# Splitting the transfers of a hybrid decoder block between SyncE's and ScalarE's DMA queues

## The chip, the cores and the metric

The kernel runs on one core of a Trainium2 chip, in one launch. The metric is the device time of the execution in microseconds (us). A core has five engines with programs of their own: TensorE (PE, with its weight loads PEld), VectorE (DVE), ScalarE (ACT), GpSimd (POOL) and SyncE (SP). Each works through its program in order. An engine's program can also hold instructions that start a DMA transfer; here they are said to stand in that engine's queue. The transfers themselves are carried out by 16 DMA engines. Engines and transfers wait for each other by semaphores.

## What is computed

The reference is one decoder block on 1024 tokens of width 1024 in float32. Two kinds of attention run on parallel head groups: A is grouped-query attention in a causal window of 128 with a sink in the softmax, 8 query heads on 2 key/value heads of 64; B mixes three dilated causal windows over 8 heads of 64. Cut to what matters:

```python
mod = cond @ w_ada + b_ada                         # cond = silu(c); six rows of 1024
sh_a, sc_a, gt_a, sh_m, sc_m, gt_m = split(mod, 6)
h = rms_norm(x, g_attn_pre) * (1 + sc_a) + sh_a
proj = h @ w_in                                    # 1024 x 2304: q, k, v of A, then of B
oa = banded_attention(rope(qa), rope(ka), va, 127, sink=sink_a)
ob = dilated_mixture_attention(rope(qb), rope(kb), vb)
y = concat(rms_norm(oa, g_mix_a), rms_norm(ob, g_mix_b)) @ w_out
x = x + gt_a * rms_norm(y, g_attn_post)
h = rms_norm(x, g_mlp_pre) * (1 + sc_m) + sh_m
y = square(relu(h @ w_up)) @ w_down                # 1024 -> 4096 -> 1024
x = x + gt_m * rms_norm(y, g_mlp_post)
```

## The kernel before

Matrices are multiplied in float32 precision out of two parts: a value is split into a high part, rounded to the type that TensorE takes, and the low part that is left, and each product is three matmuls (high by high, high by low, low by high). So each operand of TensorE is first cast by ScalarE (the high part) and subtracted by DVE or POOL (the low part).

The stages, as they start: load x and the first weights, norm and transposes; the input projection in six units (u = 0, 1 for A, 2 to 5 for B), each of which reads six blocks of w_in (128 x 512 values each); attention items, which run while later units are still projected (for A an item is one of 8 query blocks of one key/value head, in three parts: scores, exponentials and transposes, products with v); the output projection with post-norm and the input of the MLP, in eight blocks of 128 rows (the "output stage"); the MLP.

*The planner.* `Sched` fixes the order of each engine's program when the kernel is built. Each piece of work is an `op` with an engine, an estimated duration, the pieces it needs (`deps`), the buffers that it takes and gives back (`takes`, `gives`, counted by a `Res`), and a priority. The planner keeps a clock for each engine and gives out the piece that its estimates say is ready. `load` is the piece for a transfer: it stands on SyncE, its issue is priced at 0.62 us for each DMA instruction (`n`), and its end at the end of a running sum of transfer times, `self.dma`, plus 0.8. `e = op("ACT", ...)` and the like give the event that others name in their `deps`.

*The transfers.* All of the 533 DMA instructions stand in SyncE's queue. Those that matter here, by line:
- `load_w` (L530): a block of w_in, 256 KB, into the buffer `w_st`. `split_w` (L539 on ScalarE, L544 on DVE or POOL) makes `w_hl` of it, and the second of these gives `w_st` back. Unit 0's blocks are loaded in a hand-written order ahead of all (`prio is None`); the others are given a priority.
- `f_st` (L803): the rotated and split q and k of a unit go from the stage buffer `hl` to other partitions, into the tiles `qt` and `kt`. This is a transfer within the core's memory. For q of A, high and low parts are separate pieces (`s_` is 0 and 1), with one DMA instruction for each head and half in a piece. `hl` is written by L763 or L774 on ScalarE (high part) and L766 or L777 on POOL or DVE (low part). Scores (L1177 for A, L1122 for B) read `kt` and `qt`.
- `ada_piece` (L994): a piece of w_ada, 512 KB, into `wa_st`, for the modulation rows that are needed later; POOL multiplies and adds it up (L1005 to L1010). Its pieces with i below `NADA` (24) run beside the attention, the later ones in the MLP stage. L1034 and L1035 load rows of b_ada and of the post-norm's gain into `gate_st`.
- `open_attention` (L971): the masks, once.
- L1314 (A) and L1296 (B): an attention result from `ot` to `o_dram`, which the output stage reads back. `ot` (L1309, L1293 on DVE) is made out of `otmp` (L1304, L1289 on ScalarE), a copy of the products with v.
- L1343: w_out in eight pieces of 512 KB into `wo_st`. L1418 reads `o_dram` back; L1422 reads the rows of x for the residual, `x_sb2`, 512 KB.
- L1641: the raw blocks of w_up and w_down; the first four of these pairs are read in the output stage.

`wa_st`, `gate_st`, `wo_st`, `x_sb2` and `hl` are all tiles of one ring of stage buffers (`stage`, `r_stg`).

On ScalarE, in the attention stage, stand the casts of w (L539) and hl (L763, L774), copies of v (L825, `vt`; L839, `v_hl`), tables for the rotation (L721), exponentials (L1197 for A, L1148 for B), casts of transposed probabilities (`ph`, L1241) and the copies `otmp`. TensorE's projection writes `pj` (L861 to L864); it transposes v with L831 (`pv`) and the probabilities with L1227 to L1234 (`pt_ps`), and L1257 to L1269 are the products with v (`o_ps`).

## Time and profile before

| | us |
|---|---|
| median of 3 runs | 1166.8 |
| lowest and highest of them | 1165.25, 1167.23 |
| the profiled execution, whole | 1161.99 |
| its span, first to last instruction | 1160.2 |
| mean clock granted to TensorE in it | 0.986 of full speed |

| engine | work in the attention and output stages |
|---|---|
| TensorE | projections, scores, transposes, products |
| ScalarE | high parts, exponentials, copies out of the accumulators |
| DVE | rotation, low parts, maxima, sums |
| POOL | low parts, division of the probabilities, modulation rows |
| SyncE | all transfers |

The slices of the page, 29 us each, show the stages by the transfers: the line "GB/s" has 351 in the first slice, where x and the first weights come in, 102 to 182 while attention and projection run together, and then rises and falls with the blocks of the MLP.

How to read the rows that follow: times are in microseconds from the span's start, "x8" is a count, and an arrow "<-" gives what ended an idle time. SPq is SyncE's queue; a time beside it is the time that an instruction took to be issued there, its waits not counted unless they fell into it. In a chain, "DMA kt<-hl" is a transfer from its issue to its landing. PEclk is the clock granted to TensorE as a share of full speed.

### The profile page before, as it was taken

What the parts mean: (1) busy time and instruction counts of PE and PEld (TensorE: products, weight loads), DVE (VectorE), ACT (ScalarE), POOL (GpSimd) and SP (SyncE); (2) the same over time, 40 slices, a digit from 0 to 9 for tenths busy, and PEclk for the clock granted to TensorE, in tenths of its full rate; (3) what the DMA queues carried; (4) which work ended last, traced back from release to release, by engine and by line L of the source; (5) the groups of instructions that cost most, each with busy time, mean ns of one, the idle gap of its engine ahead of it and who ended that gap; (6) DMA issues with size and microseconds to landing.
All of it is one profiled execution on the core that took longest, in us unless ns stands there. A gap on an engine that the chain in (4) does not pass through costs nothing.

```text
span 1160.2 us, 15646 instructions
## 1 busy us (share of the span) xinstructions
PE 1117.1 (96%) x5416; PEld 926.6 (80%) x5416; DVE 815.4 (70%) x1380; ACT 639.2 (55%) x1105; POOL 261.1 (23%) x344
## 2 busy tenths in 40 slices
PE   8989989999999899998999999999999999999996
PEld 7768778788888787887788888888888888888885
DVE  7848576566666775658969665499653796547998
ACT  7949676455555774667676524563233732246542
POOL 2347667566663441112000000000000000000002
PEclk9989989999999989999999999999999999999998
DMA  9477857465545614554683057812369212585103
GB/s 351 161 174 168 168 120 182 111 153 122 134 102 130 156 48 139 193 181 182 257 314 118 19 207 274 315 50 89 120 220 326 106 55 73 184 306 181 37 19 146
DMA packets 90944, 185.31 MB, mean 160 GB/s; under 512 B 8432, under 2 KB 31088, under 8 KB 90864
## 3 DMA queue, kind: packets, MB, share of 16 engines
q1 hardware_dynamic: 90864, 184.30, 51.1%
q8 instruction: 43, 0.70, 0.3%
q14 instruction: 37, 0.30, 0.1%
HBM read 137.08 MB, written 28.31 MB: 143 GB/s over the span
## 4 chain that ended last, share of the span: by engine, by line
PE 70%; DVE 10%; DMA 7%; issue 4%; POOL 4%; ACT 3%; SPq 2%; DVEq 0%; POOLq 0%; ACTq 0%
PE mlp_ps L1898 16%; PE mlp_ps L1899 16%; PE mlp_ps L1897 16%; PE pj L861 3%; PE pj L864 3%; PE pj L862 3%; PE s_ps L1122 2%; PE o_ps L1257 1%; DMA wa<-in_w_ada 1%; SPq L803 1%; PE pt_ps L1227 1%; DMA wa_st<-in_w_ada 1%; DVE hw L1668 1%; PE pt_ps L1230 1%; PE s_ps L1177 1%
## 5 line engine op out<-in xcount | busy, mean ns | idle before, releaser
L1897 PE MATMUL mlp_ps<-hw 128*128 128x512 f32 x896 | 349.7, 390 | 1.2 <-ACT hw L1659 1.2
L1898 PE MATMUL mlp_ps<-hw 128*128 128x512 f32 x896 | 348.7, 389 | 1.1 <-DVE hw L1665 1.1
L1899 PE MATMUL mlp_ps<-hw 128*128 128x512 f32 x896 | 348.6, 389 | 0.0
L1897 PEld LDWEIGHTS mlp_ps<-hw 128*128 128x128 f32 x896 | 168.2, 188 | 36.8 <-ACT hw L1659 1.6
L1898 PEld LDWEIGHTS mlp_ps<-hw 128*128 128x128 f32 x896 | 168.2, 188 | 36.8 <-DVE hw L1665 1.4
L1899 PEld LDWEIGHTS mlp_ps<-hw 128*128 128x128 f32 x896 | 168.2, 188 | 34.9
L1668 DVE TENSOR_TENSOR hw<-w,hw 128x1024 fp32r<-128x1024 f32 x96 | 114.5, 1219 | 94.7 <-ACT hw L1661 94.4
L1661 ACT CAST hw<-w 128x1024 fp32r<-128x1024 f32 x96 | 97.5, 1047 | 129.8 <-PE mlp_ps L1899 97.5
L1997 POOL TENSOR_TENSOR st<-st,nhalf 128x1 f32<-128x1 f32 x8 | 7.8, 978 | 601.9 <-DVE st L1995 601.9
L861 PE MATMUL pj<-hw,w_hl 128*128 128x512 f32 x240 | 104.2, 434 | 0.0
L864 PE MATMUL pj<-hw,w_hl 128*128 128x512 f32 x240 | 95.5, 398 | 0.0
L862 PE MATMUL pj<-hw,w_hl 128*128 128x512 f32 x240 | 95.3, 397 | 0.0
L1245 DVE TENSOR_TENSOR ph<-pt_ps,ph 128x512 fp32r<-128x512 f32 (+1 forms) x110 | 69.7, 648 | 36.0 <-ACT ph L1241 35.7
L1661 ACT CAST hw<-u 128x1024 fp32r<-128x1024 f32 x48 | 48.7, 1052 | 64.6 <-PE mlp_ps L1899 64.6
L1241 ACT CAST ph<-pt_ps 128x512 fp32r<-128x512 f32 (+1 forms) x110 | 59.5, 555 | 32.1 <-PE pt_ps L1230 27.0
L1668 DVE TENSOR_TENSOR hw<-u,hw 128x1024 fp32r<-128x1024 f32 x48 | 57.0, 1218 | 18.2 <-ACT hw L1661 18.2
L1148 ACT ACTIVATE p_sb<-p_sb,mn 128x128 f32<-128x128 f32 (+3 forms) x64 | 49.7, 777 | 36.3 <-DVE mn L1141 34.9
L1955 DVE TENSOR_TENSOR yacc<-yacc,mlp_ps 128x512 f32<-128x512 f32 x96 | 62.1, 681 | 3.3 <-PE mlp_ps L1899 3.3
L1153 POOL TENSOR_SCALAR p_sb<-p_sb,den 128x128 f32<-128x128 f32 (+3 forms) x64 | 49.0, 775 | 47.8 <-DVE den L1151 44.6
L1010 POOL TENSOR_TENSOR ada_acc<-ada_acc,wa_st 128x512 f32<-128x512 f32 x42 | 55.5, 1320 | 3.5
L864 PEld LDWEIGHTS pj<-hw,w_hl 128*128 128x128 f32 x240 | 45.6, 190 | 10.7
L1473 PE MATMUL y_ps<-hw,oh 128*128 128x512 f32 x128 | 51.7, 404 | 0.0
(205 smaller groups left out, 2010.6 us busy)
## 6 DMA issues: line engine op xcount, KB each, us to landing
hw<-s_dram SPq DMA_DIRECT2D x84, 512.0 KB
wa_st<-in_w_ada SPq DMA_DIRECT2D x32, 512.0 KB
w<-in_w_up SPq DMA_DIRECT2D x32, 512.0 KB
w<-in_w_down SPq DMA_DIRECT2D x32, 512.0 KB
s_dram<-hw SPq DMA_DIRECT2D x28, 512.0 KB
w_st<-in_w_in SPq DMA_DIRECT2D x36, 256.0 KB
x_sb<-in_x SPq DMA_DIRECT2D x16, 512.0 KB
wa<-in_w_ada SPq DMA_DIRECT2D x32, 256.0 KB
```

What stands on the lines that cost most here:

```text
L861: T.matmul(ps, w[:, 0, n], h[0], start=(k == 0), stop=False)
L862: T.matmul(ps, w[:, 1, n], h[0], start=False, stop=False)
L864: T.matmul(ps, w[:, 0, n], h[1], start=False, stop=(k == KC - 1))
L1010: G.tensor_tensor(ada.acc[:, :512], ada.acc[:, :512], wa[:, j], ALU.add)
L1241: A.copy(b["ph"][:, 0, :w], b["pt"][:, :w])
L1245: V.tensor_tensor(b["ph"][:, 1, :w], b["pt"][:, :w], b["ph"][:, 0, :w].bitcast(F32), ALU.subtract)
L1661: A.copy(out[j][0], flat(src[j]))
L1668: V.tensor_tensor(out[j][1], flat(src[j]), out[j][0].bitcast(F32), ALU.subtract)
L1897: T.matmul(ps[m][:], sh, mh, start=starts and k == 0, stop=False, **kw)
L1898: T.matmul(ps[m][:], sh, ml_, start=False, stop=False, **kw)
L1899: T.matmul(ps[m][:], sl, mh, start=False, stop=k == 3, **kw)
L1955: e = op("DVE", t_dv(512), lambda: V.tensor_tensor(y(), y(), ps[m][:], ALU.add), [e, ml.e_y[tb, n]], gives=gives, prio=1)
```

## The change

103 of the DMA instructions go to ScalarE's queue (`nc.scalar.dma_start`), the others stay on SyncE's:
- `w_st` of units 1 to 5 (30);
- the high parts of A's q (20; the low parts and k stay);
- `wa_st` with i below 24 (24) and the four loads of `gate_st` among them;
- the masks (1), `wo_st` (8), `x_sb2` (8), and of the raw weights the halves with h = 0 (8).

The planner gets three kinds of transfer. "bulk" is what goes to ScalarE apart from q: it is ready `SLACK` (0.8 us) later than its needs are met, takes `ISSUE` (0.5 us) of ScalarE for each DMA instruction, and ends by the sum `self.dma`. "small" (q, k, `o_dram`, the reads of `o_dram`, the stores of x2) ends by a sum of its own, `self.few`, whichever queue it stands in. All others are priced as before. The different prices also move other pieces in the order of each engine's program a little, and which of DVE and POOL makes some of the low parts.

```diff
--- before.py
+++ after.py
@@ -149,6 +149,9 @@
 PW = 0.0
 
 
+SLACK, ISSUE = 0.8, 0.5
+
+
 class Ev:
 
     __slots__ = ("t", "eng")
@@ -181,7 +184,7 @@
         self.pe = {}
         self.launch = []
         self.seq = 0
-        self.dma = 0.0
+        self.dma = self.few = 0.0
         self.filler = None
 
     def step(self, dur, emit, deps=(), takes=(), gives=(), prio=5, after=None, kind="", n=1):
@@ -213,10 +216,11 @@
 
     def ready(self, o, e):
         t = 0.0
+        late = SLACK if e == "ACT" and o.kind == "bulk" else 0.0
         for d in o.deps:
             if d.t is None:
                 return None
-            x = d.t + lat(d.eng, e)
+            x = d.t + lat(d.eng, e) + late
             if x > t:
                 t = x
         for r, n in o.takes:
@@ -224,7 +228,7 @@
                 continue
             if len(r.free) < n:
                 return None
-            x = sorted(r.free)[n - 1]
+            x = sorted(r.free)[n - 1] + late
             if x > t:
                 t = x
         return t
@@ -236,10 +240,19 @@
             del r.free[:n]
         emit()
         end = start + dur
-        if e == "SP":
+        if e == "SP" and o.kind != "small":
             self.clk[e] = start + 0.62 * o.n
             self.dma = max(self.dma, start + 1.1) + max(dur, 0.62 * (o.n - 1))
             end = self.dma + 0.8
+        elif o.kind == "bulk":
+            self.clk[e] = start + ISSUE * o.n
+            self.dma = max(self.dma, start + 1.1) + dur
+            end = self.dma + 0.8
+        elif o.kind == "small":
+            each = 0.62 if e == "SP" else ISSUE
+            self.clk[e] = start + each * o.n
+            self.few = max(self.few, start + 1.1) + max(dur, each * (o.n - 1))
+            end = self.few + 0.8
         else:
             self.clk[e] = end
         o.ev.t = end
@@ -446,8 +459,9 @@
             return ring_r(name)
         return st.stgp.tile([P, 1024], F32, name=name, tag="stg")
 
-    def load(emit, nbytes, deps=(), takes=(), prio=5, gives=(), after=None, n=1):
-        return op("SP", nbytes / (345e3 if prio > -500 else 370e3), emit, deps, takes=takes, prio=prio, gives=gives, after=after, n=n)
+    def load(emit, nbytes, deps=(), takes=(), prio=5, gives=(), after=None, n=1, q="SP", kind=""):
+        return op(q, nbytes / (345e3 if prio > -500 else 370e3), emit, deps, takes=takes, prio=prio, gives=gives, after=after,
+                  n=n, kind=kind)
 
     def rsqrt_mean(dst, src, dep):
         box = []
@@ -527,11 +541,11 @@
     def load_w(u, i, prio=None, deps=()):
         def emit():
             t = w_raw[u, i] = prp.tile([P, 512], F32, name="w_st", tag="w_st", bufs=WS)
-            nc.sync.dma_start(t[:], w_in[6 * u + i])
+            (nc.sync if prio is None else nc.scalar).dma_start(t[:], w_in[6 * u + i])
         if prio is None:
             w_rawe[u, i] = in_turn(emit, 262144, r_wst)
         else:
-            w_rawe[u, i] = load(emit, 262144, deps, takes=[(r_wst, 1)], prio=prio)
+            w_rawe[u, i] = load(emit, 262144, deps, takes=[(r_wst, 1)], prio=prio, q="ACT", kind="bulk")
 
     def split_w(*a):
         def hi():
@@ -787,9 +801,10 @@
                 both = isb == (whose == "q")
                 nh = 2 if isb else 4 if whose == "q" else 1
                 for s_ in ((0, 1) if not both else (None,)):
+                    eng = nc.scalar if s_ == 0 and not isb else nc.sync
                     new = c == 0 and whose == "k" and s_ in (0, None)
 
-                    def f_st(s_=s_, new=new, mine=mine, whose=whose, nh=nh, both=both):
+                    def f_st(s_=s_, new=new, mine=mine, whose=whose, nh=nh, both=both, eng=eng):
                         if new:
                             if not x:
                                 ks[u] = kring.tile([P, 2, 1024], F32R, name="kt", tag="kt")
@@ -800,7 +815,7 @@
                             m_ = n_ // nh
                             for i in range(2) if both else (s_,):
                                 o = dst[64 * i + row:64 * i + row + m_].bitcast(F32)
-                                nc.sync.dma_start(o, src if both else src[:, s_])
+                                eng.dma_start(o, src if both else src[:, s_])
                     if new:
                         e_new[u, x] = Ev()
                     last = (whose == ("q" if c == 0 or not isb else "k")) and s_ in (1, None)
@@ -813,7 +828,8 @@
                     by = sum(a[1] * 2048 * (4 if both else 1) for a in mine)
                     e = load(f_st, by, [eh if s_ == 0 else el] + ([] if new else [e_new[u, x]]),
                              takes=[(r_k, 1 - x), (r_q, 1)] if new else [], prio=-12, n=len(mine) * (2 if both else 1),
-                             gives=[(r_stg, 1)] if last else [], after=after)
+                             gives=[(r_stg, 1)] if last else [], after=after, kind="small",
+                             q="ACT" if eng is nc.scalar else "SP")
                     (e_q if whose == "q" else e_k)[u, x].append(e)
         if c < 2:
             return
@@ -968,7 +984,8 @@
         r_k.give(sc.clk["PE"], NK)
         r_q.give(sc.clk["PE"], NQ)
         masks = mkp.tile([P, 1280], F32, name="masks")
-        e_mask = load(lambda: nc.sync.dma_start(masks[:], consts[:, CW_MB:CW_MB + 1280]), 655360, prio=-20)
+        e_mask = load(lambda: nc.scalar.dma_start(masks[:], consts[:, CW_MB:CW_MB + 1280]), 655360, prio=-20, q="ACT",
+                      kind="bulk")
         mask_b = masks[:, 0:1024]
         mask_a = masks[:, 1024:1280]
         sc.launch.append(feed_s)
@@ -991,9 +1008,10 @@
 
         def f_load():
             ada.raw[i] = stage("wa_st")
-            nc.sync.dma_start(ada.raw[i][:].rearrange("p (j n) -> p j n", j=2),
-                              ada_view[:, 2 * jp:2 * jp + 2, col:col + 512])
-        el = load(f_load, 524288, takes=[(r_stg, 1)], prio=20)
+            (nc.scalar if i < NADA else nc.sync).dma_start(ada.raw[i][:].rearrange("p (j n) -> p j n", j=2),
+                                                           ada_view[:, 2 * jp:2 * jp + 2, col:col + 512])
+        on = dict(q="ACT", kind="bulk") if i < NADA else {}
+        el = load(f_load, 524288, takes=[(r_stg, 1)], prio=20, **on)
 
         def f_acc():
             wa = ada.raw.pop(i)[:].rearrange("p (j n) -> p j n", j=2)
@@ -1031,9 +1049,10 @@
 
             def f_gl():
                 ada.gate[g] = t = stage("gate_st")
-                nc.sync.dma_start(t[:, 0:512], b_ada[0:1, col:col + 512].to_broadcast([P, 512]))
-                nc.sync.dma_start(t[:, 512:1024], gp[0:1, n0:n0 + 512].to_broadcast([P, 512]))
-            eg = load(f_gl, 524288, [e], takes=[(r_stg, 1)], prio=19)
+                eng = nc.scalar if on else nc.sync
+                eng.dma_start(t[:, 0:512], b_ada[0:1, col:col + 512].to_broadcast([P, 512]))
+                eng.dma_start(t[:, 512:1024], gp[0:1, n0:n0 + 512].to_broadcast([P, 512]))
+            eg = load(f_gl, 524288, [e], takes=[(r_stg, 1)], prio=19, n=2, **on)
 
             def f_g1():
                 t = ada.gate[g]
@@ -1294,7 +1313,7 @@
             e = op("ACT", t_ps(256), f_o1, [ep], takes=[(r_tmp, 1)], prio=0)
             e = op("DVE", t_dv(256), f_o2, [e], takes=[(r_ot, 1)], gives=[(r_ob, 1), (r_tmp, 1)], prio=0)
             e_o[i] = load(lambda: nc.sync.dma_start(o_dram[tp][2 + u, 64 * h:64 * h + 64], ob["ot"][:]), 65536, [e],
-                          gives=[(r_ot, 1)], prio=-5)
+                          gives=[(r_ot, 1)], prio=-5, kind="small")
         else:
             u, qb = it
             kv = u
@@ -1314,7 +1333,7 @@
                     nc.sync.dma_start(
                         o_dram[qb // 2][2 * kv + c, :, qb % 2 * P:qb % 2 * P + P].rearrange("(h d) q -> d h q", d=64),
                         ob["ot"][:, 256 * c:256 * c + 256].rearrange("d (h q) -> d h q", h=2))
-            e_o[i] = load(f_st, 131072, [e], gives=[(r_ot, 1)], prio=-5, n=2)
+            e_o[i] = load(f_st, 131072, [e], gives=[(r_ot, 1)], prio=-5, n=2, kind="small")
 
     e_o = {}
     next_item = [0]
@@ -1340,8 +1359,8 @@
         for k in range(KC):
             def f_l(k=k):
                 ph2.raw[k] = stage("wo_st")
-                nc.sync.dma_start(ph2.raw[k][:], w_out[k * P:(k + 1) * P])
-            e = load(f_l, 524288, takes=[(r_stg, 1), (r_wo, 1)], prio=-8)
+                nc.scalar.dma_start(ph2.raw[k][:], w_out[k * P:(k + 1) * P])
+            e = load(f_l, 524288, takes=[(r_stg, 1), (r_wo, 1)], prio=-8, q="ACT", kind="bulk")
             g = cols[:, 56 + k:57 + k]
 
             def f_h(k=k, g=g):
@@ -1419,11 +1438,11 @@
 
         def f_lx():
             b["xt"] = stage("x_sb2")
-            nc.sync.dma_start(b["xt"][:], x[tb * P:(tb + 1) * P])
+            nc.scalar.dma_start(b["xt"][:], x[tb * P:(tb + 1) * P])
         deps = [e_ for k_, e_ in e_o.items()
                 if (items[k_][1] if items[k_][0] > 1 else items[k_][1] // 2) == tb // 2]
-        el = load(f_lo, 524288, deps, takes=[(ph2.r_o, 1)], prio=-6)
-        ex = load(f_lx, 524288, takes=[(r_stg, 1)], prio=-3)
+        el = load(f_lo, 524288, deps, takes=[(ph2.r_o, 1)], prio=-6, kind="small")
+        ex = load(f_lx, 524288, takes=[(r_stg, 1)], prio=-3, q="ACT", kind="bulk")
 
         def f_oh():
             b["oh"] = by_k(ring_l("oh"))
@@ -1518,7 +1537,7 @@
                gives=[(r_u, 1)] if tb == TB - 1 else [], prio=1)
         e = op("DVE", t_dv(D), lambda: V.tensor_tensor(b["y"][:], b["y"][:], b["xt"][:], ALU.add), [e, ex],
                gives=[(r_stg, 1)], prio=1)
-        e_x2[tb] = load(lambda: nc.sync.dma_start(x2_dram[tb][:], b["y"][:]), 524288, [e], prio=-2)
+        e_x2[tb] = load(lambda: nc.sync.dma_start(x2_dram[tb][:], b["y"][:]), 524288, [e], prio=-2, kind="small")
         e = op("ACT", t_sb(D) + AP_COST, f_sq(2, False), [e], prio=1)
         e = norm(2, e)
 
@@ -1638,9 +1657,10 @@
                 else:
                     r0 = 2048 * r + 512 * w + 256 * j
                     src = w_down[r0:r0 + 256, 512 * c:512 * c + 512]
-                nc.sync.dma_start(two(t.b[q][j]), src.rearrange("(k p) n -> p k n", p=P))
+                (nc.sync if h else nc.scalar).dma_start(two(t.b[q][j]), src.rearrange("(k p) n -> p k n", p=P))
             deps = [halves[h - 1].e_b["T2"][j]] if h else [e_x2[2 + RAW.index(q)]]
-            t.e_b[q].append(load(emit, 524288, deps, takes=[(r_raw, 1)], prio=50 + h))
+            on = {} if h else dict(q="ACT", kind="bulk")
+            t.e_b[q].append(load(emit, 524288, deps, takes=[(r_raw, 1)], prio=50 + h, **on))
 
     def flat(x):
         return x[:] if len(x.shape) == 2 else x.rearrange("p k n -> p (k n)")
```

## The prediction

> **What bounds the kernel now.** I read the page's totals, then windows cut at the places where TensorE's share drops, then the waits of TensorE, ScalarE and SyncE's queue, and last the queue's own timeline there. The forecast is **slightly slower**, by about 0.3%.
>
> ```profile
> span 1160.2 us, 15646 instructions
> PE 1117.1 (96%) x5416; PEld 926.6 (80%) x5416; DVE 815.4 (70%) x1380; ACT 639.2 (55%) x1105; POOL 261.1 (23%) x344
> q1 hardware_dynamic: 90864, 184.30, 51.1%
> ```
>
> TensorE is busy 1117.1 of 1160.2 us, so 43.1 us is idle, and some of that is the start and the end. ScalarE's 55% is a mean and says little. All kernel transfers lie in one queue, whose packets fill half of the 16 engines' span.
>
> ```profile
> core 0: us, PE busy (x) PEld busy (x) DVE busy (x) ACT busy (x) POOL busy (x), PEclk, DMA share, GB/s
> 76.00:83.00 7.00, 1.49 (x7) 0.94 (x6) 1.55 (x3) 0.59 (x1) 0.00 (x0) 0.85 0.82 179
> 83.00:88.00 5.00, 5.00 (x18) 3.90 (x18) 3.07 (x12) 2.75 (x10) 2.00 (x4) 0.52 0.71 155
> 92.00:117.00 25.00, 24.54 (x146) 20.77 (x144) 21.57 (x71) 24.05 (x72) 21.21 (x36) 1.00 0.74 171
> 139.00:146.00 7.00, 4.68 (x27) 3.66 (x25) 2.00 (x5) 2.01 (x5) 0.80 (x1) 0.98 0.66 119
> 146.00:153.00 7.00, 4.29 (x19) 3.89 (x20) 4.46 (x15) 4.62 (x14) 6.78 (x12) 0.53 0.43 115
> 203.00:208.00 5.00, 2.48 (x15) 1.78 (x14) 1.13 (x3) 2.35 (x5) 1.74 (x2) 0.92 0.59 190
> 208.00:211.00 3.00, 3.00 (x12) 2.66 (x11) 1.84 (x3) 1.07 (x2) 2.92 (x5) 0.56 0.51 138
> 211.00:377.00 166.00, 165.29 (x949) 140.63 (x948) 107.40 (x277) 88.43 (x182) 94.19 (x98) 1.00 0.52 123
> 395.00:408.00 13.00, 8.70 (x55) 6.81 (x55) 11.88 (x29) 11.81 (x23) 8.43 (x8) 1.00 0.24 76
> 580.00:1100.00 520.00, 520.00 (x2291) 429.85 (x2291) 361.29 (x374) 247.97 (x332) 0.00 (x0) 1.00 0.47 167
> ```
>
> Each row gives the window, its length, and each engine's busy time with its count. From 580 to 1100 TensorE has no gap; nothing that the change touches can be worth time there. From 92 to 117 TensorE is nearly full (24.54 of 25), and so is ScalarE (24.05): whatever holds ScalarE there is not made up. From 211 to 377 ScalarE is busy 88.43 of 166, so it has room. After a TensorE gap the granted clock is about half: 0.52 for 5 us, 0.53 for 7, 0.56 for 3. The cost of such a stretch is its length times what is missing of the clock: 2.4, 3.3 and 1.3 us.
>
> ```profile
> PE s_ps L1177 <- DMA kt<-hl: 5.5, 1, 5.5
> PE pv L831 <- ACT tab L721: 5.0, 1, 5.0
> PE pv L831 <- DVE ot L1293: 2.9, 2, 2.5
> ACT hl L774 <- DMA qt<-hl: 7.2, 2, 4.9
> SPq L530 <- DVE w_hl L544: 23.0, 5, 8.9
> SPq L530 <- POOL w_hl L544: 19.4, 8, 6.9
> SPq L803 <- ACT w_hl L539: 11.4, 2, 8.1
> ```
>
> The columns are total, times, longest. Three TensorE stalls come from transfers: 5.5 us for kt (at 77.5), 5.0 at 143.7 (the table it names was long done; ScalarE stood 4.9 us at its cast L774, waiting for a q store to land and free its stage), and 2.5 us at 205. The prefetch w_st (L530) held SyncE's queue 23.0 and 19.4 us for its buffer, and whatever stood behind it too.
>
> **The change part by part.** Of 533 transfers 103 leave SyncE's queue: 30 w_st, 24 wa_st, 20 q stores (high parts of A), 8 wo_st, 8 x_sb2, 8 halves of w_up, 4 gate rows, 1 masks. The bytes are the same, and so is TensorE's work. ScalarE works in order, so its queue's waits now stand between its casts and exponentials. The planner sets some work in another order and gives DVE more of the splitting.
>
> ```profile
> 64.81 0.44 SPq L994 DMA_DIRECT2D wa_st<-in_w_ada  x1
> 69.31 8.35 SPq L803 DMA_DIRECT2D qt<-hl  x10
> 77.75 1.32 SPq L803 DMA_DIRECT2D kt<-hl  x2
> 79.16 7.46 SPq L803 DMA_DIRECT2D qt<-hl  x10
> 91.82 0.94 SPq L530 DMA_DIRECT2D w_st<-in_w_in  x2
> 94.86 4.33 SPq L803 DMA_DIRECT2D qt<-hl  x6
> 133.94 0.43 SPq L994 DMA_DIRECT2D wa_st<-in_w_ada  x1
> 203.74 4.40 SPq L1296 DMA_DIRECT2D o_dram<-ot  x2
> 78.45 4.46 DMA kt<-hl
> 135.32 8.68 DMA qt<-hl
> 201.62 5.50 DMA o_dram<-ot
> 94.45 0.58 ACT L1304 COPY otmp<-o_ps 64x512 f32<-64x512 f32 x1
> ```
>
> The first eight rows are issues on SyncE's queue with their count, the next three are pieces of the chain of waits (start, and time until landed), the last is a copy on ScalarE. A q store takes 0.84, 0.75 or 0.72 us to issue (8.35/10, 7.46/10, 4.33/6), a bulk load 0.43 to 0.47. No transfer is issued on ScalarE in this trace, so its price there is unknown: 0.43 is the low bound, 0.84 the high one; I take the same as on SyncE, since these are the same instructions. 103 issues cost ScalarE 20 x 0.75 + 83 x 0.45 = 52 us. In the MLP stage there is none of it.
>
> One thing of the compiled program decides the rest. There are eight completion semaphores for DMAs, dealt in turn over both queues together, and a DMA isn't issued before the one eight places earlier has landed. Before, only SyncE's queue stood for that. Now ScalarE does.
>
> *a. First attention item (77.5).* The two kt stores that end the 5.5 us stall stand behind ten q stores. Four of these go to ScalarE, so kt is issued about 4 x 0.84 = 3.3 us sooner. Against this, five q stores stand on ScalarE ahead of a copy that TensorE needs for v, and one of them has the semaphore of the wa_st issued at 64.81; and the next q stores and a wa_st stand ahead of the first exponentials. Bounds: the whole stall with its slow clock, 5.5 + 2.4 = 7.9 gained; or the copy's delay is all that comes, the 3.3 gained going the other way, 3.3 lost. I take **1.5 gained**, nearer to the middle than to either end since both rows are of the same burst.
>
> *b. ScalarE held at 94.* In the changed program four q stores and two w_st loads follow an exponential, and the copy otmp (L1304, at 94.45 before) comes after them. The first q store needs the scores of an item that TensorE reaches at about the time at which that store was issued before, 94.86. The first w_st, four places behind that store on the same queue, has the same semaphore: it waits until the store has landed. The landings shown take 4.46 to 8.68; of these 5.50 is nearest to a store that isn't behind other loads. So ScalarE is held until about 94.86 + 5.50 + 0.94 = 101.3, and the copy comes 6.8 us late. ScalarE is full until 117 and can't make it up; TensorE, in order too, has projections that need no ScalarE for a part of it. Bounds: 0 lost, if TensorE's other work covers it all; 4.46 to 8.68 lands the store at 99.3 to 103.5, which with the slow clock behind it (2.4) makes up to 94.86 + 8.68 + 0.94 - 94.45 + 2.4 = 12.4. I take **5 lost and 1.3** for a clock stretch as short as that at 208.
>
> *c. The stall at 143.7.* It is 5.0 with 3.3 of slow clock. Its q store lands after 8.68 us because it was issued behind a wa_st (133.94). On two queues it need not be, but the same q and wa_st now hold ScalarE itself, and w_st loads at about 111 to 123 wait there for POOL's release, as they waited on SyncE's (19.4 in eight). Bounds: 8.3 gained, or another hold of 4.46 lost. I take **2 gained**, the middle.
>
> *d. The stall at 205.* The output stores (4.40 for two issues, 5.50 to land) stood behind w_st and wa_st. SyncE's queue has then only small stores, so most of 2.5 + 1.3 goes. Bounds 0 and 3.8; I take **3 gained**.
>
> *e. Issues from 153 to 377.* About 45 bulk loads x 0.45 = 20 us on a ScalarE with 77.57 us idle of 166 in the largest of these windows. The work that hides it is TensorE's projections; gone that cover, 20 is lost. Below nothing is possible to the 0.7 us (166 - 165.29) that TensorE idles there. I take **2 lost**, near the end with room.
>
> *f. 395 to 408.* ScalarE sets the pace (11.81 of 13, TensorE 8.70), and four wo_st loads are issued right ahead of it: 4 x 0.45 = **1.8 lost**; bounds 0 and 1.8. The output stage's x_sb2 and w_up loads and the planner's order I put at nothing, 0 to 3 lost either way: the cover is the work of eight row blocks in turn.
>
> **Sum:** 1.5 - 5 - 1.3 + 2 + 3 - 2 - 1.8 = -3.6, so slower by 3.6 us. The profiled execution took 1161.99 (span 1160.2); it becomes 1165.6. The median of three runs is 1166.8, 4.8 above it; on that scale 1170.4, rounded up to **1171** for the holds after 153 that I left at nothing.
>
> A rule speaks about the whole of it. The Trainium skill, "DMA: Bandwidth & Descriptors", section "Issuing engines are not separate DMA queues", says that transfers started by different engines run on the same 16 DMA engines and interleave, and that several issuing engines save only sequencer time. By it, a to d would gain issue time alone; the long landing (8.68 behind one load) neither confirms nor contradicts it, as one queue was in use.
>
> **The rivals.**
> - *Faster: the freed queue wins.* Small stores never stand behind a load that waits for a buffer (23.0 + 19.4 us on L530), and landings get short enough that ScalarE's holds fall into its idle time. For it speak the three stalls, all at transfers; against it b, where the wait is on the store's own landing. It decides if landings at 94 fall under about 2.5 us. It gives (5.5 + 2.4) + (5.0 + 3.3) + (2.5 + 1.3) = 20 us with b at nothing, 1146.8; with half of it 1157.
> - *Much slower: ScalarE is held at each group of loads.* The hold of b comes again at 67, 123 and 132, four times 4.46 or more with a slow stretch of 1.3 to 3.3 each: 4 x 5.8 = 23, less d's 3, so 1187. For it: the eight semaphores; against it, from 211 on a transfer lands long before its semaphore comes round (DMA share 0.52).
> - *No change: only issue time moves.* What SyncE's queue saves at a and d (3.3 + 1.5) is spent on ScalarE in the 92 to 117 window, where ten issues at 0.45 make 4.5: within 1 us of 1166.8. Against it: ScalarE's waits are longer than its issues. This is the mechanism by which the rule of the Trainium skill named above would come out here.
>
> **How the numbers follow.** The forecast (slightly slower, 1169.2 to 1180) has 0.37, much slower 0.13, the faster rival 0.40, no change 0.10. A difference under 0.2%, 2.3 us, can't be told from none here. So slower by more 0.50, within 0.10, faster by more 0.40. The range reaches from the full gain (1147) to the four holds (1187); the likeliest case's own is 1169 to 1180.
>
> **What would show it.** Right: on ScalarE at about 94 an idle of 5 us or more ahead of the otmp copy with a DMA named, TensorE's share in 92 to 117 down by 4 us or more; the stall at 205 gone; kt's stall under 3 us. ScalarE's busy casts stay near 639 us. Wrong: TensorE's gaps at 77, 143 and 205 all gone and none new by 150 (then the faster rival), or new ScalarE holds past 211, where I put nearly nothing.

## The result, and the profile after

| | median us | lowest to highest | ratio to before (95% interval) |
|---|---|---|---|
| before | 1167.01 | 1165.25 to 1168.04 | 1 |
| changed | 1182.34 | 1177.54 to 1184.32 | 1.014 (1.0117 to 1.0163) |

The changed kernel is slower by 1.4% by the ratio; by the two medians it is 15.3 us, or 1.3%. The forecast was slower by 0.3%. The profiled execution of the changed kernel took 1184.32, with a span of 1182.5; against the one profiled before (1161.99) that is 22.3 us, so its trace shows somewhat more of the loss than the medians have. Line numbers move: L530, L803, L994, L1177, L1304 are now L544, L818, L1011, L1196, L1323; of the TensorE lines named below, L831 is now L847 and L1257 is L1276. On ScalarE the casts of hl, L763 and L774, are now L777 and L788; the copies of v, L825 and L839, are L841 and L855; the exponentials, L1148 and L1197, are L1167 and L1216.

Totals and queues on the page of the changed kernel:

```profile
span 1182.5 us, 15625 instructions
PE 1127.9 (95%) x5416; PEld 931.8 (79%) x5416; DVE 825.1 (70%) x1395; ACT 630.6 (53%) x1087; POOL 260.0 (22%) x347
q1 hardware_dynamic: 73584, 147.46, 39.2%
q10 hardware_dynamic: 17280, 36.84, 10.8%
```

A second queue, q10, is ScalarE's. TensorE does the same 5416 matmuls and is busy 10.8 us longer, at a mean granted clock of 0.980 in place of 0.986. The other 11.5 of the 22.3 us are idle time. Windows of the changed kernel, where it can be held against those of before; from about 120 on the work is 10 to 18 us later, and the cuts are moved with it:

```profile
76.00:83.00 7.00, 5.48 (x18) 3.98 (x16) 4.27 (x7) 0.63 (x2) 0.00 (x0) 0.76 0.68 132
83.00:88.00 5.00, 3.45 (x18) 3.08 (x19) 3.45 (x14) 1.34 (x3) 0.00 (x0) 0.82 0.70 123
92.00:117.00 25.00, 20.90 (x116) 17.58 (x115) 15.13 (x57) 15.74 (x52) 13.68 (x29) 0.93 0.58 112
117.00:143.00 26.00, 19.35 (x88) 14.87 (x88) 14.53 (x39) 14.17 (x41) 12.68 (x22) 0.83 0.55 141
143.00:153.00 10.00, 10.00 (x58) 8.70 (x57) 5.43 (x21) 7.18 (x23) 9.32 (x23) 0.94 0.33 86
153.00:170.00 17.00, 17.00 (x100) 14.26 (x99) 12.43 (x37) 14.17 (x38) 5.63 (x15) 1.00 0.54 143
217.00:223.00 6.00, 2.57 (x18) 2.02 (x16) 1.44 (x4) 2.61 (x6) 5.73 (x7) 0.98 0.50 165
223.00:226.00 3.00, 3.00 (x11) 2.71 (x12) 2.98 (x4) 1.06 (x2) 2.92 (x3) 0.50 0.13 25
```

From 92 to 117 both TensorE (24.54 to 20.90) and ScalarE (24.05 to 15.74) have lost work: TensorE waits for a ScalarE that is itself idle. From 117 to 143 it is the same, with a clock of 0.83. From 143 to 170 there is no idle time: the stall of before at 143.7 isn't there. The one of before at 205 is, at 217 to 223, with its slow clock (0.50) behind it. The waits of ScalarE, then its timeline, say for what:

```profile
ACT otmp L1323 <- DMA w_st<-in_w_in: 10.0, 1, 10.0
ACT v_hl L855 <- DMA qt<-hl: 7.3, 1, 7.3
ACT otmp L1323 <- DMA qt<-hl: 6.6, 1, 6.6
ACT vt L841 <- DMA qt<-hl: 6.5, 1, 6.5
ACT p_sb L1167 <- POOL w_hl L558: 3.8, 1, 3.8
ACT p_sb L1167 <- POOL ada_acc L1028: 3.7, 1, 3.7
```

```profile
67.87 6.57 ACTq L818 DMA_DIRECT2D qt<-hl  x5
77.36 6.55 ACTq L818 DMA_DIRECT2D qt<-hl  x2
96.72 4.59 ACTq L818 DMA_DIRECT2D qt<-hl  x3
101.91 1.00 ACTq L544 DMA_DIRECT2D w_st<-in_w_in  x2
102.95 0.58 ACT L1323 COPY otmp<-o_ps 64x512 f32<-64x512 f32 x1 [6.57 <-DMA qt<-hl]
130.85 6.92 ACTq L818 DMA_DIRECT2D qt<-hl  x2
137.87 0.58 ACT L1323 COPY otmp<-o_ps 64x512 f32<-64x512 f32 x1 [10.02 <-DMA w_st<-in_w_in]
```

Four waits of 6.5 to 10 us stand at groups of ScalarE's own DMA instructions, and each is followed by a copy or cast that TensorE needs. ScalarE computes nothing from a `qt` tile: it waits there only to be allowed to issue the next transfer. For what it waits, the trace's records of the semaphores tell (read from the records, not a view of the profile). The 533 DMA instructions share eight completion semaphores, 66 or 67 to each, and an instruction waits until the transfer that had its semaphore before has landed:

| waiting instruction | until | for the landing of |
|---|---|---|
| ScalarE: four q stores of the group at 67.87 | 69.74 to 73.72 | w_st, wa_st, w_st and q of ScalarE, issued at 66.49, 66.89, 67.35, 67.87 |
| ScalarE: second q store of the group at 77.36 | 83.27 | q of SyncE, issued at 75.75 |
| ScalarE: second q store of the three at 96.72 | 99.68 | q of SyncE, issued at 89.26 |
| ScalarE: w_st at 101.91 | 101.89 | q of ScalarE, issued at 96.04 |
| ScalarE: w_st at 130.41 | 130.33 | o_dram of SyncE, issued at 126.78 |
| ScalarE: second q store of the group at 130.85 | 137.12 | kt of SyncE, issued at 129.11 |

The view names one transfer for a wait made of several: the fourth hold, put down to w_st, is for stores of SyncE's. Of the 30.4 us of the four holds 10.7 are the issuing itself, 18 instructions, and the rest is waiting; the first hold is issuing for the most part (4.1 of 6.5). Two shorter waits, 3.8 and 3.7, are loads that wait on ScalarE for POOL to give a buffer back.

How late TensorE is can be followed through both traces: the start of the k-th matmul in the changed kernel minus the k-th before. The two orders differ in places, so a single value can be some us off; the plateaus are firm. Worked out from the matmul records (not a view of the profile), by the time in the kernel before:

```
before at    70   84   90   95  110  117  125  143  149  155  180  205  220  377  410  450  470  522  600
after       1.0  1.7  1.9  6.2  9.5 10.0 17.9 18.4 13.4 12.1 10.5 14.4 15.5 16.3 17.3 16.9 21.9 22.5 22.5
```

Four steps make it: +7.6 from 90 to 110, +8.4 from 117 to 143, -6.3 where the stall at 143.7 and its slow clock are gone, and +5.6 in the output stage from 450 on. From 522 on nothing is added: the MLP is not touched. The measure has a spread of its own: a run below that is no slower than the kernel before (ratio 0.9992) comes out 5.0 us late at 600, so a step much under that says little by itself.

### The profile page after: what moved, and what is told of

Same layout as the page of the kernel before. It is cut to its first block, busy times and chain, and to the rows that moved or that the text cites. A ratio compares the mean times of both kernels' runs of the same rounds, so it can differ in the third digit from the quotient of the medians.

```text
span 1182.5 us, 15625 instructions
## 1 busy us (share of the span) xinstructions
PE 1127.9 (95%) x5416; PEld 931.8 (79%) x5416; DVE 825.1 (70%) x1395; ACT 630.6 (53%) x1087; POOL 260.0 (22%) x347
## 3 DMA queue, kind: packets, MB, share of 16 engines
q10 hardware_dynamic: 17280, 36.84, 10.8%
## 4 chain that ended last, share of the span: by engine, by line
PE 70%; DVE 9%; DMA 8%; POOL 5%; issue 4%; ACT 3%; SPq 0%; ACTq 0%; DVEq 0%; POOLq 0%
PE mlp_ps L1919 16%; PE mlp_ps L1918 16%; PE mlp_ps L1917 16%; PE pj L877 3%; DMA wa_st<-in_w_ada 3%; PE pj L880 3%; PE pj L878 3%; PE s_ps L1141 2%; DMA o_sb<-o_dram 2%; POOL ada_acc L1028 2%; PE o_ps L1276 1%; DMA qt<-hl 1%; PE pt_ps L1246 1%; DVE hw L1688 1%; POOL wa_st L1027 1%
## 5 line engine op out<-in xcount | busy, mean ns | idle before, releaser
L877 PE MATMUL pj<-hw,w_hl 128*128 128x512 f32 x240 | 105.3, 439 | 1.9 <-ACT vt L841 1.9
L880 PE MATMUL pj<-hw,w_hl 128*128 128x512 f32 x240 | 97.0, 404 | 0.0
L878 PE MATMUL pj<-hw,w_hl 128*128 128x512 f32 x240 | 96.7, 403 | 0.0
L1167 ACT ACTIVATE p_sb<-p_sb,mn 128x128 f32<-128x128 f32 (+3 forms) x64 | 49.7, 777 | 49.3 <-DVE mn L1160 37.9
```

Of the source, the lines that this page charges most:

```text
L877: T.matmul(ps, w[:, 0, n], h[0], start=(k == 0), stop=False)
L878: T.matmul(ps, w[:, 1, n], h[0], start=False, stop=False)
L880: T.matmul(ps, w[:, 0, n], h[1], start=False, stop=(k == KC - 1))
```

## The experiments

What each theory says: H, ScalarE is held by its own DMA instructions, above all by q stores; O, the new order of work by the planner's new prices; I, issue time; L, that any other order than the one before has its own stalls. "Lanes", in one of the expectations, are the completion semaphores. Ratios are to the kernel before, run on the same chip in the same call. Where one run changes prices alone or queues alone, the order of computing on every engine is the same as in the kernel that it is held against.

**The new order, all transfers on SyncE.** Prices and order of the changed kernel, with no transfer on ScalarE:

```diff
-            (nc.sync if prio is None else nc.scalar).dma_start(t[:], w_in[6 * u + i])
+            nc.sync.dma_start(t[:], w_in[6 * u + i])
...
-                nc.scalar.dma_start(ph2.raw[k][:], w_out[k * P:(k + 1) * P])
+                nc.sync.dma_start(ph2.raw[k][:], w_out[k * P:(k + 1) * P])
```

> The changed kernel's planner with all of its new prices, and so its order of work, but every transfer is put back on SyncE's queue. Theory H (holds): ScalarE is slow because it stands in order behind DMA instructions that wait for one of the eight completion semaphores; without DMAs on ScalarE the time goes back to 1162 to 1172 us, and ScalarE has no idle of over 5 us between 60 and 140 that a transfer ends, but the one at the cast of hl. Theory O (order): the new order of the engines' programs makes the loss; the time stays at 1176 to 1186. Theory I (issue time): what ScalarE loses is the time of issuing 103 DMAs; the time goes back as under H.

Measured: 1179.2 us, ratio 1.0133 (1.011 to 1.0155). As good as all of the loss is there with no DMA on ScalarE. H and I fall as explanations of the sum; O stands. (The loads keep the places that the planner gave them for a second queue, so the 1.33% is the price of this order on one queue, waits of the queue included.) The loss isn't at the same places, though. Windows of this run, then SyncE's queue in it:

```profile
core 0: us, PE busy (x) PEld busy (x) DVE busy (x) ACT busy (x) POOL busy (x), PEclk, DMA share, GB/s
60.00:145.00 85.00, 73.98 (x392) 60.98 (x391) 55.25 (x155) 53.39 (x149) 47.41 (x90) 0.94 0.68 150
145.00:160.00 15.00, 7.93 (x45) 6.23 (x43) 5.80 (x16) 6.64 (x17) 2.46 (x5) 0.84 0.38 86
```

```profile
152.99 0.33 SPq L1053 DMA_DIRECT2D gate_st<-in_b_ada  x1
155.30 1.25 SPq L818 DMA_DIRECT2D qt<-hl  x2
```

and of the queue's waits (total, times, longest):

```profile
SPq L1053 <- PE ptab L733: 10.0, 1, 10.0
```

The same two windows of the changed kernel:

```profile
60.00:145.00 85.00, 68.58 (x330) 54.97 (x329) 46.27 (x132) 42.74 (x120) 37.10 (x66) 0.88 0.62 138
145.00:160.00 15.00, 15.00 (x88) 12.83 (x87) 10.21 (x31) 12.14 (x33) 10.03 (x26) 1.00 0.42 107
```

In the same order, the queue on ScalarE costs TensorE 5.4 us of work before 145 (73.98 to 68.58, and 0.06 of the clock) and saves 7.07 after it (7.93 to 15.00). By the start of the same matmuls the changed kernel is 12.5 us behind this run at 143 (18.4 and 5.9 late) and 2.9 behind at 155 (12.1 and 9.2). The saving is what the change can do: with one queue, q stores at 155.30 stand behind a gate load that waited ten us for a stage buffer, and TensorE waits 7.8 us for q; with two, they don't.

**q back on SyncE, in planner and queue.**

```diff
-                    eng = nc.scalar if s_ == 0 and not isb else nc.sync
+                    eng = nc.sync
```

> The changed kernel with the 20 stores of the high parts of A's q back on SyncE, in the planner too; the 83 bulk loads stay on ScalarE. H: three of the four long holds (6.5, 7.3 and 6.6 us at 68, 77 and 97) are q stores waiting on each other's and on SyncE's landings, so they go, and of the 18 us that TensorE is late at 143 some 10 go: 1168 to 1175. I: 20 issues of 0.75 us are 15 of 52 us of issue time, so about 29% of the loss of 15.3 goes: 1177 to 1179. O: 1176 to 1186.

Measured: 1175.78, ratio 1.0102 (1.0081 to 1.0123). Just above H's range, below I's and, by 0.2 us, below O's. TensorE is 8.3 us late at 143 in place of 18.4, as H had it; but the order is another one too, so it tells little by itself.

**q alone on ScalarE, in planner and queue.** All other lines as before the change, but for the small prices.

```diff
-            w_rawe[u, i] = load(emit, 262144, deps, takes=[(r_wst, 1)], prio=prio, q="ACT", kind="bulk")
+            w_rawe[u, i] = load(emit, 262144, deps, takes=[(r_wst, 1)], prio=prio)
...
-        on = dict(q="ACT", kind="bulk") if i < NADA else {}
+        on = {}
```

> The reverse: the 20 stores of the high parts of A's q stay on ScalarE, all bulk loads are back on SyncE, in the planner too. H: the holds at 68, 77 and 97 stay since q stores alone follow each other on eight semaphores, 4 to 7 us each: 1173 to 1181. I: 29% of the loss, 1171 to 1173. Rival B (the bulk loads make it, by waiting for buffers on ScalarE): 1164 to 1170.

Measured: 1175.09, ratio 1.0102 (1.0077 to 1.0126). Within H's range, above I's and B's. Of the three holds that H named, the first is there (the copy vt waits 8.3 us at q stores); a cast of hl at 85.5 waits 4.9, and there is none at 97. Together with the run before it: the two parts of the change lose 1.02% each and 1.4% together, so they don't add. An order is not the sum of its changes.

**The output stage's 24 loads alone.** As the last one, with q back as well, and `wo_st`, `x_sb2` and the halves of w_up left on ScalarE.

> Only the output stage's 24 loads (wo_st, x_sb2, the first halves of w_up) stay on ScalarE; q, w_st, masks, wa_st and gate_st are back on SyncE, in the planner too. H: nothing is held up to 360; the loss at 450 to 470 (the cast oh waits 8.4 us for o_sb there) is of this part if it is made by these loads: TensorE late by 4 to 6 us, 1168 to 1173. If that loss only follows from the earlier ones, 1165 to 1169. I: 24 x 0.45 = 11 of 52 us, 1169 to 1171.

Measured: 1168.77, ratio 1.0046 (1.0028 to 1.0064). The median is in both of H's ranges, so the place decides: worked out as in the table above, TensorE is 5.2 us late at 180, long before any of these loads (the first is issued at 368), and 7.0 at 522. As far as this measure goes, the loss is again one of order.

**The old order, the queue alone.** The kernel before with its prices; 103 instructions issue from ScalarE.

```diff
-            nc.sync.dma_start(t[:], w_in[6 * u + i])
+            (nc.sync if prio is None else nc.scalar).dma_start(t[:], w_in[6 * u + i])
...
-                                nc.sync.dma_start(o, src if both else src[:, s_])
+                                (nc.scalar if s_ == 0 and not isb else nc.sync).dma_start(o, src if both else src[:, s_])
```

> The reverse of the first run: the planner of the kernel before, with its prices and so the same order of computing on every engine, but the 103 transfers issue from ScalarE's queue, at the places where they stood among SyncE's. H: ScalarE stands for completion semaphores that its own and SyncE's stores hold, more than in the changed kernel since the planner allows no time for it: 1175 to 1195 us. O (the loss is made by the order): 1160 to 1168, and the three stalls at 77, 143 and 205 get shorter.

Measured: 1168.76, ratio 1.002 (0.9999 to 1.0041): no loss that can be told from none, though just above O's range. The three stalls are shorter, as O had it: 4.84, 0.36 and 1.84 us in place of 5.51, 5.02 and 2.52. But one of 2.81 has come at the scores (L1177) at 140, ended by DVE, where before had none. H as first put (q stores on ScalarE hold it, 1175 to 1195) falls for this order. ScalarE's queue in this run:

```profile
68.45 2.00 ACTq L803 DMA_DIRECT2D qt<-hl  x2
72.07 3.21 ACTq L803 DMA_DIRECT2D qt<-hl  x2
76.31 0.65 ACTq L803 DMA_DIRECT2D qt<-hl  x1
78.19 1.29 ACTq L803 DMA_DIRECT2D qt<-hl  x2
96.90 0.64 ACTq L803 DMA_DIRECT2D qt<-hl  x1
97.58 0.62 ACTq L803 DMA_DIRECT2D qt<-hl  x1
100.51 0.81 ACTq L803 DMA_DIRECT2D qt<-hl  x1
101.36 0.71 ACTq L803 DMA_DIRECT2D qt<-hl  x1
```

The same stores come one or two at a time, with ScalarE's compute between them. The trace has one idle time of 7.1 us that a q store ends, ahead of a cast of hl at 84.8; in the kernel before, ScalarE idled 6.5 us ahead of the same cast, for DVE. The holds of the changed kernel at vt, v_hl and otmp aren't there.

**A price changed by 3%.** All on SyncE, the kernel before with

```diff
-            self.clk[e] = start + 0.62 * o.n
-            self.dma = max(self.dma, start + 1.1) + max(dur, 0.62 * (o.n - 1))
+            self.clk[e] = start + 0.60 * o.n
+            self.dma = max(self.dma, start + 1.1) + max(dur, 0.60 * (o.n - 1))
```

> The kernel before, every transfer on SyncE, with one price of the planner changed by 3%: a DMA issue on SyncE costs 0.60 us in its estimates and not 0.62. The work is the same and the order of some of it moves. Theory L (the order before is a fitted one, and any other order is worse by its own stalls): 3 to 12 us above the kernel before. O in its narrow form (it is the new prices' meaning, such as the slack of 0.8 us and the sum of its own for small stores, that makes a worse order): within 3 us of the kernel before.

Measured: 1171.17, ratio 1.004 (1.0017 to 1.0063), 4.7 us on that chip's 1166.12. Nothing in this price has to do with ScalarE. L is right in that a price without any meaning for the change costs about a third of the change's loss (0.2 to 0.6% of 1.4).

**The small prices alone.** The changed kernel with all 103 back on SyncE in the planner as well. Beside the small prices, only the count of two instructions for a gate load is left of the new prices.

> The changed kernel with all 103 transfers back on SyncE in the planner as well; what is left of the change is the pricing of q, k, o_dram, o_sb and x2 as small ones, with a running sum of their own. If this pricing makes the worse order: 1168 to 1176. If it is what the planner believes of ScalarE that makes it: 1163 to 1167. L: 1167 to 1176, as for any price.

Measured: 1168.61, ratio 1.0023 (1.0007 to 1.004). The median is in two of the ranges, 1168 to 1176 and 1167 to 1176, at their low ends; by the ratio it is 2.7 us. So the sum for small stores by itself makes at most a small part of the loss. The rest of the 1.33% is there only when the planner also believes that ScalarE issues.

**The old order, bulk loads alone on ScalarE**, without q:

> As the one that changes the queue alone (planner and order of the kernel before), but the 20 stores of A's q stay on SyncE, 83 loads issue on ScalarE. H: the holds at q stores are gone, what is left is ScalarE waiting at w_st for POOL and at semaphores of SyncE's stores: 1164 to 1176 us, at least 6 below the one with q. O: as that one. I (issue time): 83/103 in number and 37 of 52 us of issue time, so 70% of that one's loss.

Measured: 1170.87, ratio 1.004 (1.0021 to 1.0058). A miss for H, which had it at least 6 us below the run with q: it is 2.1 above. O (to 1168) and I (70% of that run's loss) miss as well, since the loss is twice as large. One place shows what a load can do there:

```profile
255.82 0.34 ACTq L530 DMA_DIRECT2D w_st<-in_w_in  x1
256.20 0.59 ACT L839 CAST v_hl<-pv 128x512 fp32r<-128x512 f32 x1 [2.21 <-PE pj L864]
268.94 0.47 PE L1227 MATMUL pt_ps<-head,p_sb 128*128 128x128 f32 x1 [2.77 <-POOL p_sb L1153]
```

The load of w_in waits on ScalarE until POOL gives its buffer back at 255.8, and the cast behind it is held 2.2 us, though the view names TensorE. POOL's low parts need ScalarE's high parts and come later too, and TensorE then stalls 2.77 us for POOL's division, 0.56 before. From 256 to 264, in the time of the kernel before, TensorE's lateness grows by 3.6 us. In the run with all 103 the same load holds 2.2 us, the stall is 2.19, and 3.2 us are lost.

**The old order, q alone on ScalarE.**

```diff
-                                nc.sync.dma_start(o, src if both else src[:, s_])
+                                (nc.scalar if s_ == 0 and not isb else nc.sync).dma_start(o, src if both else src[:, s_])
```

> Planner and order of the kernel before; only the 20 stores of A's q issue from ScalarE. Taken from the two runs in that order (all 103 on ScalarE 0.20% above, 83 without q 0.40% above): if the parts add, q alone is worth -0.2%, 1163 to 1166 us, with TensorE's stalls at 77 and 143 shorter by 1 to 3 us and no idle of ScalarE over 4 us that a q store ends outside of 76 to 85. H in its first form (q stores on ScalarE hold it wherever they are): 1170 to 1176, as with the new prices.

Measured: 1164.29, ratio 0.9992 (0.9977 to 1.0006). The first form of H is out. It is the lowest of all tried, and can't be told from the kernel before. In it the two stalls are shorter, as expected: TensorE's gap at the first item is 3.4 us (5.51 before), the one at 147 is 2.7 (5.02). A hold of 6.7 at hl and one of 2.7 at otmp are there too. At the latter a q store waits until 100.91 for one that was issued at 94.63; a stall of TensorE of 2.33 us follows, and its lateness grows by 4.4 us from 95 to 110. So a hold like the forecast's b can come in the old order too, in small.

**The new order, only q's instructions back on SyncE.** The order of computing is that of the changed kernel on every engine.

```diff
-                                eng.dma_start(o, src if both else src[:, s_])
+                                nc.sync.dma_start(o, src if both else src[:, s_])
```

> The changed kernel's planner and order, its 83 bulk loads on ScalarE, and only the instructions of the 20 q stores put back on SyncE. H: the holds of 6.5, 7.3 and 6.6 us and the wait for lanes at 130 go; TensorE is then late by 5 to 9 us at 143 instead of 18.4, as it is in the same order with all on SyncE (5.9); and the time is 1168 to 1175. If the holds cost nothing in the end (they only take the place of other stalls): 1177 to 1183, and stalls for kt, qt come in their place before 160.

Measured: 1172.63, ratio 1.0062 (1.0048 to 1.0076), in H's range. ScalarE's waits of this run:

```profile
ACT hl L788 <- DMA qt<-hl: 10.1, 2, 5.5
ACT oh L1450 <- DMA o_sb<-o_dram: 7.8, 4, 6.3
ACT otmp L1323 <- DMA wa_st<-in_w_ada: 5.7, 1, 5.7
ACT hl L788 <- POOL ada_acc L1028: 5.6, 2, 4.7
```

The holds at vt, v_hl and otmp that q stores made are gone; one at bulk loads (5.7) is left, and hl waits for its stage as it does in the kernel before. TensorE is 11.5 us late at 143 in place of 18.4 (H said 5 to 9) and 9.6 at 600 in place of 22.5. So in this order, q's place in ScalarE's queue costs 1.014 - 1.0062 = 0.78%, some 9 us; and the bulk loads' place there saves 1.0133 - 1.0062 = 0.71%, some 8 us. By the intervals of the ratios each of these two is known to about 0.3%.

**The planner's slack at 0.**

```diff
-SLACK, ISSUE = 0.8, 0.5
+SLACK, ISSUE = 0.0, 0.5
```

> The changed kernel with one price of its planner altered: the slack of 0.8 us for bulk loads on ScalarE is 0. If the slack makes the worse order: 1167 to 1174. If the loads are then placed before their buffers are free and hold ScalarE: 1184 to 1195. L (any order other than the fitted one has its own stalls): anywhere within 1168 to 1186, over 3 us from the changed kernel in either direction, with its stalls at other places.

Measured: 1194.28, ratio 1.024 (1.0224 to 1.0256), in the range of loads placed too early and above L's. But its longest holds of ScalarE are not for buffers alone:

```profile
ACT vt L841 <- DMA kt<-hl: 8.7, 1, 8.7
ACT p_sb L1216 <- DMA qt<-hl: 5.6, 1, 5.6
ACT hl L788 <- DMA kt<-hl: 5.3, 1, 5.3
ACT otmp L1323 <- POOL ada_acc L1028: 5.2, 1, 5.2
```

Three of these four are landings of stores, one is POOL giving a buffer back.

**More slack, and q on SyncE.** An attempt at a version that beats both.

```diff
-SLACK, ISSUE = 0.8, 0.5
+SLACK, ISSUE = 1.6, 0.5
...
-                                eng.dma_start(o, src if both else src[:, s_])
+                                nc.sync.dma_start(o, src if both else src[:, s_])
```

> The changed kernel with the instructions of the 20 q stores back on SyncE (0.62% above the kernel before so far) and the planner's slack for bulk loads on ScalarE at 1.6 us in place of 0.8. Theory W (with q gone, what is left of the loss is bulk loads that wait on ScalarE for a buffer or a semaphore; slack buys them off, as 0 to 0.8 bought 1% with q on ScalarE): 1160 to 1168 us, and ScalarE's waits of 5.6 us for POOL at hl and 5.7 for wa_st at otmp are gone. L (every order has its own stalls): 1168 to 1182, with stalls of TensorE over 2 us at two or more new places.

Measured: 1191.13, ratio 1.0233 (1.0201 to 1.0265). W falls. The loss is beyond L's range but of L's kind, with stalls of TensorE over 2 us at several places (10.4 at 76, 5.3 at 114, 7.8 at 163). A wait of TensorE, and one of ScalarE:

```profile
PE ptab L733 <- ACT tab L735: 9.5, 3, 7.8
```

```profile
ACT tab L735 <- POOL ada_acc L1028: 11.3, 1, 11.3
```

No version tried beats the kernel before by more than its interval.

The parts, laid side by side as ratios to the kernel before:

| order of work | all on SyncE | bulk on ScalarE | q on ScalarE | both |
|---|---|---|---|---|
| before | 1 | 1.0040 | 0.9992 | 1.0020 |
| changed | 1.0133 | 1.0062 | not run | 1.0140 |

By the rows, the whole move costs 0.20% in the old order and 0.07% in the new one, neither clear of nothing. By the columns, the new order costs 1.33% with all on SyncE and 1.20% with both parts on ScalarE, but with the bulk loads alone there only 0.22%, which the intervals can't tell from none. So the parts don't add, and neither the order nor a part of the queue has a price of its own: the bulk loads cost 0.40% in the old order and save 0.71% in the new one.

## Why the prediction was right, and where it wasn't

The sign was right and the size, 3.6 us, was a quarter of the 15.3 measured. The sign was right in part by luck, as the end of this account shows. Taken by its steps, with TensorE's lateness from the table above (of a profiled pair that differs by 22.3):

- *a, first item, 1.5 gained.* Wrong in sign. Its stall for q and k fell from 5.51 to 3.07 us, as kt moved forward; but the copy of v was held 6.46 us at 68 (TensorE then waited 1.99 us for it), and the cast v_hl 7.3 at 84. Lateness at 84 is 1.7, so 1.5 gained became 1.7 lost, within the bounds.
- *b, ScalarE held at 94, 5 lost and 1.3 of clock.* Right, mechanism included: the first w_st waits for the q store four places before it, which lands after 5.85 us (5.50 was forecast). The copy otmp comes at 102.95 after 6.57 us of idle that a q store's landing ends; 101.3 was forecast. TensorE loses 7.6 us from 90 to 110; 6.3 was forecast. ScalarE's busy time stayed near 639 (630.6), so no computing was added.
- *c, the stall at 143.7, 2 gained.* The stall and its slow clock went (6.3 back by 155), but the hold at 130 that ends with 10.02 us of idle at otmp took 8.4 ahead of it. 2 gained became 2.1 lost, within the bounds.
- *d, the stall at 205, 3 gained.* Wrong. The same transpose of v, at 223 now, waits 3.43 us in place of 2.52, still for an `ot` whose store to o_dram hadn't landed. No bulk load stands in SyncE's queue there, but one still holds it, as the rows below the list show: a kt store (L818) needs the semaphore of a wa_st that ScalarE issued at 213.20, and waits for its landing at 219.01. The stores of `ot`, whose values were ready at 215.77, stand behind that kt store. The forecast had used the shared semaphores for what holds ScalarE and not for what holds SyncE. Lateness goes from 14.4 at 205 to 15.5.
- *e, issues from 153 to 377, 2 lost.* The size is near (12.1 at 155, 16.3 at 377, 4.2 in all, of which 1.1 is d's). What makes it in the changed kernel wasn't settled. In the old order there is a loss of 3.2 us in this stretch, and it comes of a load that waits for its buffer, not of issue time.
- *f, 395 to 408, 1.8 lost.* About none: lateness is 16.3 at 377 and 16.9 at 450. The output stage, put at nothing with bounds of 3, lost 5.6.

The chain of waits at d, with the issue on SyncE's queue and the product at its end:

```profile
213.20 5.81 DMA wa_st<-in_w_ada
219.02 0.55 SPq L818 DMA_DIRECT2D kt<-hl  x1
220.32 2.06 DMA o_dram<-ot
222.98 1.12 PE L847 MATMUL pv<-head,vt 128*128 128x128 f32 x4 [3.43 <-DVE ot L1312]
```

The price of an issue on ScalarE, taken from SyncE's rows, held: 0.72 us for a q store and 0.40 for a load in the mean, 47.8 us in all where 52 was reckoned.

The largest step that failed is the one that had no term: "the planner's order I put at nothing, 0 to 3 lost either way". The order by the new prices costs 1.33% with no transfer moved at all, and it decides what the parts of the queue are worth: q on ScalarE is worth 0.08% gained in the old order, which can't be told from none, and 0.78% lost in the new one. The hold of b is real in the changed kernel, but it isn't a property of the queue alone. It takes the queue and an order that puts a copy or cast, for which TensorE is waiting, right behind stores whose semaphores are still in flight; groups of two were enough (at 77.36 and 130.85). And the queue's gain came at another place than the forecast had it: bulk loads off SyncE no longer hold the small stores behind them while they wait for a buffer, 0.71% in the new order. In that order the loss by q and the gain by the bulk loads cancel to 0.07%, and the loss of the kernel is there with both or with neither.

This is why the sign was luck in part. In the old order the whole queue costs 0.20% (-0.01 to 0.41), 2.6 us by the medians: near the 3.6 of the sum, but without the hold of b. That the changed kernel is slower by more than that came with the term put at nothing.

Of the signs that the forecast named, ScalarE's idle ahead of the otmp copy came (6.57). The fall of TensorE's share in 92 to 117 (3.64 where 4 was named) and the stall at the first item (3.07 where under 3 was) missed narrowly, and the stall at 205 stayed. Two holds of ScalarE past 211 came, which were named as a sign against it: the 3.7 us at 213.7 and the 3.8 at 327.7, both at loads that wait for POOL.

The rival with holds at each group named 67, 123 and 132 beside 94; holds came at 68, 77, 97 and 130. It had the places better than the forecast, and with 1187 it was nearer to the 1182 measured than 1171 was. Its reason was wrong as a whole account, since with no transfer on ScalarE at all the loss is as large. The faster rival lost on b and d, and the rival of no change had the queue's net effect right but not the order's.

The rule of the Trainium skill, "DMA: Bandwidth & Descriptors", section "Issuing engines are not separate DMA queues", allows several issuing engines to save sequencer time only, which it calls usually small. In the new order the bulk loads' move saves some 8 us, and the trace of the run with all on SyncE shows how this fits: what is saved is time on the sequencer, but it is time of waiting in order (ten us behind a gate load), not of issuing (0.33). In the old order the same move costs 0.40%.

Two things stay open. Which of the planner's terms for ScalarE makes its order worse wasn't settled: a slack of 0 and one of 1.6 (the latter without q on ScalarE) both gave worse orders than 0.8, by 1.0% and 1.7% of the nearest runs. And the 5.6 us lost in the output stage have no cause shown. In the same order with q on SyncE TensorE loses 1.2 from 450 to 600, with the output stage's loads alone on ScalarE 1.9, and both have all 24 of these loads on ScalarE. In that stage of the changed kernel ScalarE waited 10.6 us for o_sb:

```profile
ACT oh L1450 <- DMA o_sb<-o_dram: 10.6, 3, 8.4
```

So x_sb2 and w_up in ScalarE's queue don't make the loss by themselves; what is left is the state in which the stage is entered, or the spread of single executions (the profiled one is the longest of four that lie 6.8 us apart).

## What to carry to other kernels

A DMA instruction in a compute engine's queue is a wait in that engine's program: look at what semaphore it needs, and count the whole landing of the transfer that had this semaphore before, in whichever queue, not the issue. The same holds the other way: a load moved off SyncE can still hold SyncE's stores by its semaphore. In a kernel whose order is fixed by a planner, change the queue with the old order kept and the order with the old queue kept, before the two together; else a price that has moved the order is taken for the cost of the queue. A price changed by 3% and nothing else is a cheap control: here it was worth 0.4%, so no smaller gain of a single new order says anything of its idea.

## What the runs showed of the hardware

The two queues share their completion semaphores. The 533 DMA instructions of either kernel use eight, dealt in turn in the order of the program. 525 of them use one again, and 508 of these name it in a wait in the changed kernel (500 before). So a kt store of SyncE could hold ScalarE until 137.12, and a load of ScalarE could hold SyncE until 219.01.

Loads on ScalarE's queue did not land much later as a rule. By the last update of the semaphore of each, the 24 wa_st took 4.6 us from issue to landing in the median before and 4.9 after, and the w_st from 50 us on 4.9 and 5.0. The longest wa_st grew, from 8.9 to 11.8 us. The chain of waits shows such long ones (11.47 at 88.40, 11.77 at 309.61) beside ordinary ones (5.51 at 189.29, 5.81 at 213.20).

The executions of one kernel differ more than the first three showed: 31 of the kernel before in one call lie between 1162.57 and 1173.65, 0.9%, where the three shown with the profile spanned 0.2%. So the difference of one profiled pair is uncertain by some us, as the 5.0 us of the run with q alone in the old order show.
